# Forget-gate bias and causal mask by vector passes, and a planner that sees whole PSUM banks

## The chip, the cores and the metric

The kernel runs on one core of one Trainium2 chip. The metric is the time of one execution on the device in microseconds; the kernel before takes 2558.85 us, the median of three runs between 2553.24 and 2562.44. One further execution was profiled, and all rows below are from it.

## What is computed

One inference step of a four-layer encoder for 512 prompt frames and 64 sample frames side by side (576 columns), with a model width of 1024 and 16 heads of 64. Layer 0 and layer 3 mix with a gated linear recurrence, layer 1 with sliding-window attention (SWA) with a relative bias, layer 2 with "forgetting" attention (FoX). Each layer ends in a squared-ReLU feed-forward network (FFN) of width 4096. The change is about the scores of FoX:

```
logf = log_sigmoid(proj_f + b_f)
c    = cumsum(logf)                                   # per head, along the frames
s    = einsum('bqhd,bshd->bhqs', q, k) * SCALE
s    = s + c[q] - c[k]                               # forget bias: a column for the query, a row for the key
s    = where(kpos <= qpos, s, -inf)                  # causal mask
p    = softmax(s);  o = p @ v
```

The sample's 64 frames see 128 cached keys and their own 64, with a running sum of their own.

## The kernel before

Activations lie as 128 features by frames. Each projection is a sum of three fp32r products (high times high, high times low, low times high), so weights arrive by DMA as fp32 (`ws`), ACT rounds them to `wh`, and DVE or POOL forms the rest `wl`. A projection step is 24 products into one PSUM bank.

The program doesn't issue instructions directly. Every operation is recorded by `Plan.add` (L241) with its operands, and at the end `Plan.run` and `Plan.simulate` (L335) put all of them in an order by a list schedule: each operation has a latest time derived from the order of PE's products, a cost from `Plan.cost` (L280), possible engines (`alts`), and predecessors. A predecessor is an earlier operation that touched overlapping bytes of the same tile: `Plan.region` (L233) gives partitions and columns, so two operations on different columns of one PSUM bank are independent in the plan. PE may take a product up to 48 places ahead. `Plan.emit` (L459) issues each operation; this is why nearly all rows of the trace name line 471. The framework below adds the semaphores.

PSUM has eight banks, two for each of the names `pm`, `s`, `t` and `pv`. During attention, projections use `pm` alone, `s` takes scores, `t` transposes, `pv` the values. Attention runs beside the projections of later heads: each time so much projection time has passed (4320 ns in FoX), `_att` (L1581) takes one step, and a unit passes through four of them: its score products (`qk`), then maximum (`mx`), exponential (`ex`) and scaling (`sc`), then transposes and their copies (`transp`, `tevac`), then the value products (`av`). On PE one step makes a block: the scores of a new unit, the transposes of the unit two steps older, the values of the one three steps older.

FoX (`fox`, L1899) has eight head pairs with three units each, named after their query blocks of 128: unit (3) with 512 keys for each of two heads; unit (2, 0) with 384 and 128 keys for each head, side by side in one bank per head; unit (1) with 256 keys for each head and the sample's 256 columns for both heads in the first bank. In `qk` (L2033) each region is opened by a product of four rows, `CL` times `CR` (`cl`, `cr` in the trace; the cumulative sums as high and low parts, and ones), which writes c[q] - c[k]; for the sample `SL` times `SR` with six rows. Then come three score products, and an identity times `cmr` adds the mask on the last 128 columns. The row operands come from a DRAM scratch (`crow`) by six small DMAs a pair (`prep`, L1998) and are rounded to fp32r in `prep2` (L2009). `mx` (L2059) reduces each region from PSUM to its negated maximum on DVE; `ex` (L2067) reads PSUM again for the exponential with a running sum; `sc` scales head 0 on DVE and head 1 on POOL.

SWA (`unit`, L1766) adds its bias in another way: one DVE instruction reads the scores from PSUM and the bias from SBUF, writes the sum to SBUF and gives its maximum (`CUSTOM_DVE_ANT_0` in the trace, with a read of the accumulator after it).

Of the kernel before, what the change touches and what calls it, by code (L numbers as in the profile page):

```python
# [7 lines left out]
F32 = mybir.dt.float32  # L8
F32R = mybir.dt.float32r
# [122 lines left out]
class Engine:  # L132
# [5 lines left out]
    def __getattr__(self, op):  # L138
        core, load, names = self._c, self._l, self._names

        def call(out, *a, **k):
# [15 lines left out]
            core.plan.add([(e, op) for e in names], out, a, k, outs, ins, n)  # L157
# [3 lines left out]
class Queue:  # L161
# [3 lines left out]
    def dma_start(self, out, src):  # L165
# [8 lines left out]
        self._c.plan.add([("sync", "dma_start")], out, (src,), {}, [out], [src], n)  # L174


class Core:
# [8 lines left out]
    def any(self, *names):  # L186
        return Engine(self, *names)

# [23 lines left out]
class Item:  # L212
    __slots__ = ("alts", "out", "a", "k", "n", "pe", "pred", "succ", "tiles", "late", "at", "wait", "end", "seq", "func", "r32", "cols")


class Plan:
# [24 lines left out]
    def add(self, alts, out, a, k, outs, ins, n):  # L241
        o = Item()
        o.alts, o.out, o.a, o.k, o.n, o.seq = alts, out, a, k, n, len(self.items)
# [9 lines left out]
        for x, w in rw:  # L253
# [6 lines left out]
            p0, p1, runs = self.region(x)  # L260
# [19 lines left out]
    def cost(self, o, alt):  # L280
        e, op = alt
# [9 lines left out]
        if op == "scalar_tensor_tensor":  # L291
            return 1.85 * n + 90.0
        return (6.8 if op == "reciprocal" else 1.35) * n + 100.0
# [41 lines left out]
    def simulate(self):  # L335
# [15 lines left out]
        def offer(o):  # L351
            for e, _ in o.alts:
                cand[e].append(o)
# [17 lines left out]
        while left:  # L371
# [7 lines left out]
            again = True  # L379
            while again:  # L380
                again = False
                for e in names:
# [8 lines left out]
                    for o in cand[e]:  # L391
                        if e == "tensor" and o.seq > last:
                            continue
                        if o.at > now:
                            soon = o.at if soon is None else min(soon, o.at)
                            continue
                        k = (o.late + (1500.0 if o.func and o.func != func[0] else 0.0), o.seq)
# [10 lines left out]
                    if len(o.alts) > 1 and e == "gpsimd":  # L408

                        v = max(free["vector"], now) + self.cost(o, o.alts[0])  # L410
                        for x in cand["vector"]:
                            if x is not o and x.at <= now and x.late <= o.late and gets(x):
                                v += self.cost(x, x.alts[0])
                        if v <= now + c:
                            soon = max(free["vector"], now + 50.0)
                            heapq.heappush(heap, (soon, count, None))
                            count += 1
                            continue
# [1901 lines left out]
```

## Time and profile before

| | before |
|---|---|
| median of three runs | 2558.85 us |
| profiled execution: time, span | 2560.35 us, 2558.6 us |
| mean granted clock of the tensor engine | 0.983 |
| PE, PE weight loads | 98%, 95% of the span |
| DVE, ACT, POOL | 67%, 47%, 40% |
| DMA | 213 MB, 83 GB/s on average |

PE is the tensor engine's products, PEld its weight loads, DVE the vector engine, ACT the scalar engine, POOL GpSimd, SP the engine whose queue issues all DMAs. A share of the whole span says little about one stage, so the stages are read from views of stretches. A row of the timeline gives the start of the first instruction of a group, the time to the end of its last, what it computes, and in brackets the idle time before it and what released it. Starts are what to compare: products overlap, so that one lasts about 0.3 us while the next begins 0.1 us after it.

### The profile page before, as it was taken

The page shows a single profiled execution, that of the slowest core. Times are in us where ns is not written, and L with a number is a line of the kernel's source. Part 1 is how long each engine was busy: PE and PEld are TensorE (multiplying, and loading weights), DVE is VectorE, ACT ScalarE, POOL GpSimd, SP SyncE. Part 2 cuts the span into 40 slices and gives each one's busy share as a digit, 9 for nine tenths or more (in the row PEclk, how much of TensorE's full clock was granted, in tenths as well). Part 3 has the DMA queues.
Part 4 walks back from the last instruction along what each step waited for, and adds up shares of the span by engine and source line. Part 5 has one row for each costly group of instructions (what it writes and reads, how often), then busy time and mean ns, then how long its engine had stood idle before and what let it go on. Part 6 is the DMA issues. An engine that isn't in the chain of part 4 may idle for free. (4 is left out here: it accounts for less than half of the span.)

```text
span 2558.6 us, 47679 instructions
## 1 busy us (share of the span) xinstructions
PE 2503.4 (98%) x18897; PEld 2442.8 (95%) x18897; DVE 1711.8 (67%) x2835; ACT 1207.4 (47%) x2648; POOL 1015.9 (40%) x1084
## 2 busy tenths in 40 slices
PE   9999999999999999999999999999999999999998
PEld 9999999998789999999888889999999999999998
DVE  7776658676667575586643357586596796576584
ACT  6854435344554353463533334353463784353461
POOL 5644325343333252364312123253263763253260
PEclk9999999999999999999989889999999999999998
DMA  5135223242121222232321121232241231222231
GB/s 184 59 117 94 89 83 108 75 132 76 56 71 42 67 96 82 88 125 78 92 63 50 57 80 34 66 100 83 83 142 59 70 103 60 67 100 83 83 100 38
DMA packets 72687, 213.18 MB, mean 83 GB/s; under 512 B 9512, under 2 KB 24224, under 8 KB 72464
## 3 DMA queue, kind: packets, MB, share of 16 engines
q1 hardware_dynamic: 72464, 210.14, 26.5%
q8 instruction: 148, 2.42, 0.4%
q14 instruction: 75, 0.61, 0.1%
HBM read 199.16 MB, written 10.95 MB: 82 GB/s over the span
## 5 line engine op out<-in xcount | busy, mean ns | idle before, releaser
L471 DVE TENSOR_TENSOR wl<-ws,wh 128x512 fp32r<-128x512 f32 x548 | 476.3, 883 | 151.2 <-ACT wh L471 114.7
L471 ACT ACTIVATE wh<-ws 128x512 fp32r<-128x512 f32 x684 | 412.8, 625 | 322.2 <-PE pv L471 83.0
L471 POOL TENSOR_TENSOR q<-u 128x288 f32<-128x288 f32 x256 | 222.0, 872 | 259.1 <-ACT u L471 258.9
L471 POOL TENSOR_TENSOR wl<-ss,wh 128x512 fp32r<-128x512 f32 x72 | 117.6, 1634 | 501.5 <-PE pv L471 227.3
L471 POOL TENSOR_TENSOR wl<-ws,wh 128x512 fp32r<-128x512 f32 x136 | 202.5, 1495 | 212.6 <-ACT wh L471 142.3
L471 ACT ACTIVATE wh<-ss 128x512 fp32r<-128x512 f32 x192 | 119.7, 630 | 206.4 <-DVE ss L471 86.0
L471 PE MATMUL pm<-xh,wh 128*128 128x288 f32 x688 | 206.8, 301 | 0.2 <-DVE ol L471 0.2
L471 PE MATMUL pm<-xh,wl 128*128 128x288 f32 x688 | 205.5, 299 | 0.0
L471 PE MATMUL pm<-xl,wh 128*128 128x288 f32 x688 | 205.4, 299 | 0.0
L471 PE MATMUL pm<-hl,wh 128*128 128x288 f32 x520 | 154.0, 296 | 0.3 <-DVE hl L471 0.2
L471 PE MATMUL t<-hl,wh 128*128 128x288 f32 x520 | 153.5, 295 | 0.4 <-DVE hl L471 0.4
L471 PE MATMUL t<-hh,wl 128*128 128x288 f32 x520 | 153.8, 296 | 0.0
L471 PE MATMUL t<-hh,wh 128*128 128x288 f32 x520 | 153.6, 295 | 0.0
L471 PE MATMUL pm<-hh,wh 128*128 128x288 f32 x520 | 153.6, 295 | 0.0
L471 PE MATMUL pm<-hh,wl 128*128 128x288 f32 x520 | 153.4, 295 | 0.0
L471 PE MATMUL t<-xh,wh 128*128 128x288 f32 x504 | 149.6, 297 | 1.2 <-ACT xh L471 1.2
L471 PE MATMUL t<-xl,wh 128*128 128x288 f32 x504 | 149.6, 297 | 0.2
L471 PE MATMUL t<-xh,wl 128*128 128x288 f32 x504 | 149.1, 296 | 0.0
L471 PE MATMUL s<-hh,wl 128*128 128x288 f32 x504 | 149.0, 296 | 0.0
L471 PE MATMUL s<-hl,wh 128*128 128x288 f32 x504 | 148.8, 295 | 0.2 <-DVE hl L471 0.2
L471 PE MATMUL pv<-hh,wh 128*128 128x288 f32 x504 | 148.8, 295 | 0.0
L471 PE MATMUL pv<-hh,wl 128*128 128x288 f32 x504 | 148.7, 295 | 0.0
(434 smaller groups left out, 8801.1 us busy)
## 6 DMA issues: line engine op xcount, KB each, us to landing
ws<-w SPq DMA_DIRECT2D x365, 512.0 KB
toep_d<-toep SPq DMA_DIRECT2D x1, 3064.0 KB
res<-x SPq DMA_DIRECT2D x8, 288.0 KB
o_fxk<-kf SPq DMA_DIRECT2D x8, 288.0 KB
bt<-toep_d SPq DMA_DIRECT2D x16, 128.0 KB
o_fxv<-v SPq DMA_DIRECT2D x16, 128.0 KB
o_y<-res SPq DMA_DIRECT2D x2, 576.0 KB
o_y<-res SPq DMA_DIRECT2D x4, 288.0 KB
```

Source lines behind the costliest of these rows:

```text
L471: getattr(getattr(self.nc, e), op)(real(o.out), *[real(x) for x in o.a], **{n: real(x) for n, x in o.k.items()})
```

## The change

1. FoX: the bias products and the mask products go. The negated cumulative sums are written to DRAM once and loaded per pair as rows spread over 128 partitions (`nb`: two of 512 columns, one of 256), and the queries' sums are transposed once into columns (`cq`). In `qk`, ACT or POOL writes `nb` plus the column of `cq` into the unit's `pt`, and POOL adds the mask there. `mx` becomes the instruction of SWA: scores plus `pt` into `pt`, with the maximum, and a small negation. `ex` then reads `pt` from SBUF in place of PSUM.
2. The plan: for a PSUM operand, any access covers all partitions and all columns of its tile.
3. The plan: some operations may go to other engines than before (copies DVE or ACT; scaling DVE, ACT or POOL; squares ACT or POOL), an operation with a choice is put off where another of its engines would end it sooner, and the cost figures are new.

```diff
+    def copy(self, out, x):
+        self.alt(out, ("vector", "tensor_copy", (x,), {}), ("scalar", "activation", (x, AF.Copy), {}))
+    def add_col(self, out, x, col):
+        self.alt(out, ("scalar", "activation", (x, AF.Identity), {"bias": col}),
+                 ("gpsimd", "tensor_tensor", (x, col.to_broadcast(list(out.shape))), {"op": ALU.add}))
+    def mul_col(self, out, x, col):
...
+    def square(self, out, x):
...
@@ Plan.add
-            p0, p1, runs = self.region(x)
+            p0, p1, runs = (0, P, [(0, 1 << 20)]) if x.space == PSUM else self.region(x)
@@ Plan.cost
-            return 1.02 * n + 110.0 + (95.0 if "accum_out" in o.k else 0.0)
+            return 1.02 * n + (100.0 if o.bank else 130.0) + (190.0 if "accum_out" in k else 0.0)
-            return 2.5 * n + 120.0 if op == "tensor_tensor" else 1.2 * n + 100.0
+            return 2.7 * n + 120.0 if op == "tensor_tensor" else 1.2 * n + 120.0
...
-        return (6.8 if op == "reciprocal" else 1.35) * n + 100.0
+        if o.bank:
+            return 1.2 * n + 110.0
+        return (1.85 if op == "scalar_tensor_tensor" else 1.45) * n + 110.0
@@ tevac
-        self.nc.scalar.activation(u["pt"][0][:, :n[0]], u["t"][0][:, :n[0]], AF.Copy)
-        self.nc.vector.tensor_copy(u["pt"][1][:, :n[1]], u["t"][1][:, :n[1]])
+        for h in range(2):
+            self.nc.copy(u["pt"][h][:, :n[h]], u["t"][h][:, :n[h]])
@@ fox, ftask
+            nc.sync.dma_start(crow[:, 0:TP], ng[:16, :])
+            nc.sync.dma_start(crow[:, TP:768], ngs[:16, :256])
...
+            def tq():
+                g.append(self.paux())
+                for t in range(5):
+                    src = cc[:16, P * t:P * t + P] if t < 4 else lc[:16, 0:P]
+                    nc.tensor.transpose(g[0][:, 16 * t:16 * t + 16], src, self.ident[:16, :16])
+            self.later(tq, lc[:16, :P])
+            while not g:
+                yield
@@ prep
+            nb[p] = [self.slot("nb") for _ in range(2)] + [self.half("nbs")]
             for h in range(2):
-                nc.sync.dma_start(raw[0][c0:c0 + 2, :TP], two[h, :, :TP])
-                nc.sync.dma_start(raw[1][c0 + 2:c0 + 4, :TP], two[h, :, :TP])
...
+                row = crow[2 * p + h:2 * p + h + 1]
+                nc.sync.dma_start(nb[p][h][:, :TP], row[:, :TP].to_broadcast([P, TP]))
+                nc.sync.dma_start(nb[p][2][64 * h:64 * h + 64, :256], row[:, TP:768].to_broadcast([64, 256]))
@@ qk
-                            nc.tensor.matmul(o[h], CL[cb, qb], CR[cb, :w], start=True, stop=False)
-                            nc.tensor.matmul(o[h][:, w - P:], identr, cmr[:, 0:P], start=False, stop=True)
-                        nc.tensor.matmul(o, SL[cb, :P], SR[cb, :256], start=True, stop=False)
-                        nc.tensor.matmul(o[:, P:], identr, cmr[:, P:256], start=False, stop=True)
...
+                            nc.add_col(d, nb[p][h][:, :w], cq[:, j:j + 1])
+                            d, m = d[:, w - P:], cm[:, 0:P]
+                        nc.gpsimd.tensor_tensor(d, d, m, op=ALU.add)
@@ mx, ex
-                        nc.vector.tensor_reduce(nm[:, i:i + 1], u["s"][h][:, c0:c0 + w], axis=mybir.AxisListType.X,
-                                                op=ALU.max, negate=True)
+                        nc.vector.tensor_tensor_reduce(d, u["s"][h][:, c0:c0 + w], d, 1.0, NEG, ALU.add, ALU.max,
+                                                       accum_out=top[:, i:i + 1])
+                    nc.vector.tensor_scalar(nm[:, :len(ops)], top[:, :len(ops)], -1.0, None, op0=ALU.mult)
-                        nc.scalar.activation(pt[h][:, c0:c0 + w], u["s"][h][:, c0:c0 + w], AF.Exp, bias=nm[:, i:i + 1],
+                        nc.scalar.activation(pt[h][:, c0:c0 + w], pt[h][:, c0:c0 + w], AF.Exp, bias=nm[:, i:i + 1],
```

## Rows read from the trace of the kernel before

**Rows 1.** The page, part 1: busy us, share of the span, instructions of each engine.

```profile
PE 2503.4 (98%) x18897; PEld 2442.8 (95%) x18897; DVE 1711.8 (67%) x2835; ACT 1207.4 (47%) x2648; POOL 1015.9 (40%) x1084
```

**Rows 2.** Busy time by stretch: FoX, then sliding-window attention; last columns clock, DMA, GB/s.

```profile
1240.00:1530.00 290.00, 275.25 (x2049) 242.48 (x2049) 133.02 (x274) 113.57 (x305) 63.53 (x95) 0.91 0.19 60
...
590.00:760.00 170.00, 154.35 (x1279) 138.34 (x1278) 107.87 (x390) 83.94 (x276) 63.75 (x105) 0.96 0.20 61
```

**Rows 3.** Timeline of PE in a block of unit (2, 0).

```profile
1347.11 0.44 PE L471 MATMUL s<-cr,cl 4*128 4x384 f32 x2
1347.48 0.44 PE L471 MATMUL s<-kh,qh 64*128 64x384 f32 x2
...
1348.57 0.33 PE L471 MATMUL s<-cr,cl 4*128 4x128 f32 x2
1349.54 0.33 PE L471 MATMUL s<-kh,qh 64*128 64x128 f32 x2 [0.65 <-DVE nm L471]
...
1350.63 0.33 PE L471 MATMUL s<-kh,ql 64*128 64x128 f32 x1 [0.55 <-DVE nm L471]
```

**Rows 4.** Timeline of DVE in the same block.

```profile
1348.92 0.56 DVE L471 TENSOR_REDUCE nm<-s 128x1 f32<-128x384 f32 x1 [5.44 <-PE s L471]
1350.02 0.56 DVE L471 TENSOR_REDUCE nm<-s 128x1 f32<-128x384 f32 x1 [0.54 <-PE s L471]
```

**Rows 5.** Waits of PE (us in total, times, longest): FoX, then sliding-window attention.

```profile
PE s L471 <- DVE nm L471: 12.0, 21, 0.7
PE s L471 <- ACT pt L471: 2.0, 3, 0.7
...
PE s L471 <- DVE mx L471: 9.4, 20, 0.8
```

**Rows 6.** Timeline of PE in a block of unit (3).

```profile
1338.57 0.50 PE L471 MATMUL s<-cr,cl 4*128 4x512 f32 x2
1339.00 0.50 PE L471 MATMUL s<-kh,qh 64*128 64x512 f32 x2
...
1339.88 0.44 PE L471 MATMUL s<-cmr 128*128 128x128 f32 x2
1340.16 1.06 PE L471 MATMUL t<-ident,pt 128*128 128x128 f32 x8
```

**Rows 7.** Timeline of PE in a block of unit (1) with the sample, without a stop.

```profile
1328.92 0.38 PE L471 MATMUL s<-cr,cl 4*128 4x256 f32 x2
1329.23 0.39 PE L471 MATMUL s<-kh,qh 64*128 64x256 f32 x2
...
1329.78 0.44 PE L471 MATMUL s<-cmr 128*128 128x128 f32 x2
1330.15 0.38 PE L471 MATMUL s<-sr,sl 6*128 6x256 f32 x1
1330.46 0.55 PE L471 MATMUL s<-kcs,qs 128*128 128x128 f32 x3
```

**Rows 8.** Busy time by stretch: block of unit (3), after the block of rows 3, later.

```profile
1338.50:1342.20 3.70, 3.70 (x37) 2.65 (x35) 2.34 (x4) 1.79 (x5) 0.80 (x1) 1.00 0.60 213
1353.50:1355.50 2.00, 2.00 (x11) 1.99 (x10) 1.03 (x2) 0.09 (x1) 0.95 (x2) 0.50 0.00 0
1356.00:1358.00 2.00, 2.00 (x19) 2.00 (x18) 0.00 (x0) 0.00 (x0) 0.00 (x0) 1.00 0.19 66
```

**Rows 9.** Groups by form in FoX: busy us, mean ns, idle before and releaser.

```profile
L471 ACT ACTIVATE pt<-s,nm 128x256 f32<-128x256 f32 x24 | 11.2, 470 | 18.6 <-PE s L471 13.8 <-DVE nm L471 4.7
...
L471 DVE TENSOR_REDUCE nm<-s 128x1 f32<-128x256 f32 x24 | 9.4, 421 | 22.1 <-PE s L471 20.0 <-ACT pt L471 2.1
...
L471 POOL TENSOR_TENSOR pt<-pt,den 128x256 f32<-128x256 f32 x8 | 5.2, 656 | 23.6 <-DVE den L471 23.6
```

**Rows 10.** Groups by form in sliding-window attention.

```profile
L471 DVE CUSTOM_DVE_ANT_0 pt<-s,bt 128x256 f32<-128x256 f32 x48 | 18.8, 421 | 13.6 <-PE s L471 11.7 <-POOL qs L471 1.4
...
L471 DVE DVE_READ_ACCUMULATOR2_ANT mx<- 128x1 f32 x80 | 6.6, 82 | 0.0
```

More of the change, by code (lines that the diff above doesn't have):

```diff
@@ L156, in call @@
             load.account(outs, ins, end, name)
-            core.plan.add([(e, op) for e in names], out, a, k, outs, ins, n)
+            core.plan.add([(e, op, a, k) for e in names], out, outs, ins, n)
         return call
@@ L212 @@
 class Item:
-    __slots__ = ("alts", "out", "a", "k", "n", "pe", "pred", "succ", "tiles", "late", "at", "wait", "end", "seq", "func", "r32", "cols")
+    __slots__ = ("alts", "out", "n", "bank", "pe", "pred", "succ", "tiles", "late", "at", "wait", "end", "seq", "func", "r32", "cols")
 class Plan:
@@ L239, in region, with add @@
         return p0, p1, Load.region(None, x)[1]
-    def add(self, alts, out, a, k, outs, ins, n):
+    def add(self, alts, out, outs, ins, n):
         o = Item()
-        o.alts, o.out, o.a, o.k, o.n, o.seq = alts, out, a, k, n, len(self.items)
+        o.alts, o.out, o.n, o.seq = alts, out, n, len(self.items)
+        a, k = alts[0][2:]
+        o.bank = any(x.space == PSUM for x in ins)
         o.pe = alts[0][0] == "tensor"
@@ L280, in cost @@
     def cost(self, o, alt):
-        e, op = alt
+        e, op, _, k = alt
         n = o.n
@@ L407, in simulate @@
                     c = self.cost(o, alt)
[L408 to L416, printed above, removed]
+                    if len(o.alts) > 1:
+                        wait = None
+                        for y in o.alts:
+                            f = y[0]
+                            if f == e:
+                                continue
+                            v = max(free[f], now) + self.cost(o, y)
+                            if v <= now + c:
+                                for x in cand[f]:
+                                    if x is not o and x.at <= now and x.late <= o.late and gets(x):
+                                        v += self.cost(x, next(z for z in x.alts if z[0] == f))
+                            if v < now + c or v == now + c and f == "vector":
+                                wait = max(free[f], now + 50.0)
+                                break
+                        if wait is not None:
+                            heapq.heappush(heap, (wait, count, None))
                             count += 1
+                            skip.add((e, o))
+                            again = True
                             continue
@@ L1303, in copy @@
         def copy(out, src, n):
[L1304 to L1307 removed]
+            nc.copy(out, src)
         def uev(m):
```

119 lines of the change are left out of this document (59 added, 60 removed).

## Prediction

> **What bounds the kernel now.** I read the page first: the tensor engine, PE, is busy for 2503.4 of 2558.6 us [rows 1], so 55.2 us of idle time are all that a better order alone can give, besides work taken away and clock won back. Then the busy time by stretch: of those 55.2 us, the sliding-window attention stage holds 170 - 154.4 = 15.6 and the FoX stage 290 - 275.3 = 14.8; in the same two the granted clock is 0.96 and 0.91 of full speed [rows 2]. The rest, 24.8 us, is spread over the other 2100 us. So the two attention stages are where something can be won, and in both PE is still the bound: in FoX, VectorE (DVE) is busy 133 us of 290, ScalarE (ACT) 114, GpSimd (POOL) 64.
>
> The timeline of PE then shows what an attention block between two projections looks like. In the block of unit (2, 0) PE starts the bias pair of the 384-column region, its products, the mask pair, the bias pair of the 128-column region, and then stands twice, 0.65 and 0.55 us, "released by DVE nm" [rows 3]. The timeline of DVE says why: the reduction of the first region in one bank runs from 1348.92 to 1349.48, that in the other from 1350.02 to 1350.58, and PE starts its next product into that bank 0.05 to 0.06 us later [rows 3, 4]. PE waits for a reader of other columns of the bank that it is about to write. The planner compares columns, sees no conflict, and puts the reduction ahead of the remaining products; the program's semaphores make PE wait. The list of waits has 24 such stops in FoX (12.0 + 2.0 us) and 20 with "DVE mx" in the sliding-window stage (9.4 us) [rows 5].
>
> **Products taken away.** Per head pair 18 products go (8 bias, 8 mask, one bias and one mask for the sample), 144 in all. I take each pair's price from start to start of its group and the next. Unit (3): 1339.00 - 1338.57 = 0.43 and 1340.16 - 1339.88 = 0.28, together 0.71 us [rows 6]. Unit (2, 0): 0.37 for the 384-column bias [rows 3], 0.37 for a mask pair that another bias follows (1330.15 - 1329.78, [rows 7]), and 0.28 each for the 128-column bias (the wait hides its own price; the 128-column mask pair is nearest) and the last mask: 1.30. Unit (1) with the sample: 0.31 + 0.37 + 0.31 [rows 7] and half of 0.28 for a single mask: 1.13. That is 3.14 us a pair, 25 us for eight. Bounds: the 3968 columns that go per pair at the pace of an undisturbed stretch (19 products of 256 columns in 2.00 us, [rows 8]: 0.41 ns a column) would be 1.6 us a pair, 13 in all; above, 27, since some of them ran at the lower clock. I take 25, which is read directly.
>
> **Waits.** With a bank counted as a whole, the reduction can't be placed between two products of its bank: it follows the last one, on DVE, and PE doesn't meet it. All 44 stops are of this kind by their releaser, 23.4 us. Each also costs the refilling of the pipe: 1349.54 - 1348.57 = 0.97 less 0.28 for the pair is 0.69 against 0.65 of idle time. With 0.06 each I take 26 us, with bounds of 18 (a third of them come back elsewhere) and 28.
>
> **Clock.** Two levels are granted, 1.0 (2.4 GHz) and 0.5 (1.2 GHz). A mean of 0.91 over 290 us is 52 us at the lower one, 0.96 over 170 is 14, 66 together [rows 2]. At the lower level 11 products start in 2 us, at the upper 19 [rows 8], so 42% of such time is lost: 28 us. Behind the two stops of [rows 3] a stretch runs at 0.50, while the block of unit (3), which has transposes and value products but no stop, keeps 1.00 throughout [rows 6, 8]. So I expect most falls to go with the stops and take three quarters, 21 us; the bounds are 0 and 28.
>
> One rule speaks against this. The Trainium skill (TensorE: Matmul & The Clock Gate, Part 4: PE-mode transpose) says that transposes don't count as activity for the clock gate; by it the transposes in each block would pull the clock down whether or not PE stopped, and the sum would be 21 us smaller. The undisturbed block of unit (3), with its eight transposes at 1.00, speaks for the stops instead.
>
> **What is added.** For each of 72 regions: bias plus cq (ACT or POOL), the mask on 128 columns (POOL), and in place of the reduction a pass that adds the bias and takes the maximum. That pass exists in the sliding-window stage: 421 ns for 256 columns from PSUM, the reduction of today also 421, plus 82 for reading its accumulator [rows 9, 10]: 72 x 0.08 = 6 us on DVE. The bias adds are 2816 columns a pair, 11 x 0.470 [rows 9] = 5.2 us, 41 us if all are on ACT, which idles for 176 of 290. The masks are at most 72 x 0.656 = 47 us on POOL, idle for 226. None of it needs a product of PE, so it can run before its block; I cost it at nothing on PE. If that cover were gone it is the chain of the fourth case. The exponential now reads SBUF, so the banks come free one step earlier. What leaves: the casts and the row operands.
>
> **Queues.** On SP's queue the six small row loads a pair become four broadcast loads of 640 KB together. At the 213 GB/s that the queues carried beside a block [rows 8] that is 3.0 us a pair of 36 us. The loads are issued two units ahead; a weight load queued behind them is late by up to these 3 us, and with a mean of 60 GB/s in the stage [rows 2] the queue has room to make that up: nothing. The five transposes for cq and the wait for them let attention start one or two pumps later, with projections running meanwhile; it returns as units left over at the end. I take 3 us, from 0 to 6. Products, copies and squares that get another engine, and the new cost figures, act where PE is already full: nothing, and at best a third of the 24.8 us outside, 8.
>
> **Sum.** 25 + 26 + 21 - 3 = 69 us. The profiled execution took 2560.35, 1.5 above the median of the runs, so 2560 - 69 = 2491, and by the median 2490 us.
>
> **Rivals.**
> First, the clock stays as it is: the falls belong to the blocks with their small products, not to the stops. Then 25 + 26 - 3 = 48: 2511 us. For it: falls lie only in attention stages. Against: unit (3).
> Second, the plan doesn't do what it says, and PE waits as long as before: the maximum now starts only after the bank's last product and a vector-built operand, and PE meets it at the next block's products into the same two banks or at the transposes. Then the clock stays too: 25 - 3 = 22, 2537 us. It takes a maximum that ends a whole block late, some 235/24 = 9.8 us after its products (235 is the FoX stage less its 55 of the sum); for four regions of 256 columns it takes 4 x (421 + 82) ns = 2 us. Against it.
> Third, slower: the vector chain of a unit (bias, mask, maximum, exponential, scaling) becomes the bound of FoX. Transposes come two blocks after the products, so it decides from 2 x 9.8 = 19.6 us; from there each us costs 24 us, and after the 69 won the change is slower by 0.3% from 19.6 + 77/24 = 22.8. At 23.6 it would be 2490 + 96 = 2586 us. What the rows give is 2.0 + 4 x 0.470 + 4 x 0.656 = 6.5 us plus hand-overs [rows 9, 10]; it would have to queue three times as long as it works. The Trainium skill (SBUF — State Buffer, Who interferes with whom) says that a DVE instruction with two SBUF inputs and a GpSimd instruction that reads SBUF block one another; the added masks would meet the weight subtractions of DVE, which is how such a queue could grow. No row here separates the two.
>
> **Chances and range.** Forecast 0.70, clock stays 0.16, waits stay 0.10, slower 0.03, some other loss near today's time 0.01. Low end: 27 + 28 + 28 - 0 and 8 from elsewhere is 91, or 2468. The high end takes in the second figure, 2511, and half of the way from there to the waits that stay: 2526. Left out: the third and fourth cases and some 0.05 beyond the ends. A change within 0.3%, about 8 us, can't be told from none here; faster than that are the first three cases all but a remnant, 0.95; the same 0.02; slower 0.03.
>
> **What would show it.** In the changed profile: no waits of PE for "DVE nm", "mx" or "top" in either stage; no products from cl, cr, sl, sr or cmr; a mean clock in FoX of 0.97 or more, and a stage of about 235 us instead of 290. If the waits go and the clock stays near 0.91, the first rival is right; if PE waits at transposes for pt, the third. The forecast falls if PE's stops move to other releasers in like number.

## The result and the profile after

The changed kernel takes 2461.53 us (median of four runs, 2460.81 to 2461.68) against 2559.77 for the kernel before: a ratio of 0.9619, 95% interval [0.9601, 0.9638], 98 us less. The forecast was 2490 us with a range from 2468 to 2526. The sign and the three mechanisms of the gain were right. A fourth term, put down as a small loss, turned out to be a gain, and with it the time lies below the range.

The page, part 1, against [rows 1] (all calls go through one helper, which stands at L518 here and at L471 before):

```profile
PE 2431.0 (99%) x18758; PEld 2395.3 (97%) x18758; DVE 1645.6 (67%) x2840; ACT 1309.4 (53%) x2914; POOL 917.7 (37%) x1019
```

The span is 2459.9 us, so PE's idle time fell from 55.2 to 28.9 us, and its busy time by 72.4 us. The first is the waits; the second holds both the products taken away and the clock.

To compare stages I bound them by products that all kernels have: the sliding-window stage from its first score product to the 25th product of the next FFN (its first into a bank of `t`), FoX from the transpose of the forget gate to the last product with a cached value. Busy time by stretch between these marks (PE, PEld, DVE, ACT, POOL busy with their counts, then clock, DMA share, GB/s), first the kernel before:

```profile
622.90:916.10 293.20, 279.10 (x2231) 262.61 (x2231) 192.65 (x523) 128.34 (x362) 102.59 (x139) 0.98 0.19 58
1241.20:1528.90 287.70, 273.39 (x2031) 240.91 (x2033) 131.31 (x270) 112.74 (x302) 62.99 (x94) 0.91 0.19 59
```

and the changed kernel:

```profile
627.90:894.80 266.90, 264.81 (x2231) 254.49 (x2231) 175.85 (x493) 151.46 (x419) 84.02 (x112) 1.00 0.20 64
1217.70:1431.80 214.10, 214.05 (x1882) 198.37 (x1884) 114.92 (x327) 142.37 (x365) 94.44 (x180) 1.00 0.33 103
```

FoX loses 73.6 us: PE stands for 0.05 us of 214 where it stood for 14.3, and the clock is full where it was 0.91. The sliding-window stage, whose code is the same, loses 26.3 us.

The timeline of PE in a block of unit (3) and one of unit (2, 0), which answer to [rows 6] and [rows 3]:

```profile
1297.44 0.50 PE L518 MATMUL s<-kh,qh 64*128 64x512 f32 x2
...
1298.34 1.09 PE L518 MATMUL t<-ident,pt 128*128 128x128 f32 x8
...
1305.42 0.44 PE L518 MATMUL s<-kh,qh 64*128 64x384 f32 x2
1305.70 0.34 PE L518 MATMUL s<-kl,qh 64*128 64x384 f32 x2
1305.88 0.34 PE L518 MATMUL s<-kh,ql 64*128 64x384 f32 x2
1306.05 0.22 PE L518 MATMUL s<-kh,qh 64*128 64x128 f32 x2
1306.11 0.28 PE L518 MATMUL s<-kl,qh 64*128 64x128 f32 x2
1306.22 0.27 PE L518 MATMUL s<-kh,ql 64*128 64x128 f32 x2
1306.43 0.88 PE L518 MATMUL t<-ident,pt 128*128 128x128 f32 x6
```

No bracket, so no idle time. The scores of unit (2, 0) take 1.01 us from start to the first transpose where they took 4.06 (1347.11 to 1351.17 in the block of [rows 3]); those of unit (3) take 0.90 where they took 1.59 [rows 6]. VectorE in the same block, against [rows 4]:

```profile
1306.63 0.56 DVE L518 CUSTOM_DVE_ANT_0 pt<-s,pt 128x384 f32<-128x384 f32 x1 [4.22 <-PE s L518]
...
1308.13 0.17 DVE L518 TENSOR_SCALAR nm<-top 128x4 f32<-128x4 f32 x1
```

The first pass over a bank now follows the last product of the block (1306.22 + 0.27 = 1306.49). The maxima are done 1.6 us later, well ahead of the next block. Against [rows 5], the largest waits of PE that are left in the whole kernel are single ones in the recurrent layers; in the sliding-window stage there are 2.1 us, in FoX 0.05, and none in the list names `mx`, `nm` or `top`:

```profile
PE t L518 <- ACT gt L518: 2.1, 2, 1.1
PE s L518 <- ACT gt L518: 2.0, 1, 2.0
```

The added work in FoX, in groups by form, against [rows 9]:

```profile
L518 ACT ACTIVATE pt<-nb,cq 128x512 f32<-128x512 f32 x15 | 10.4, 713 | 0.0
...
L518 ACT ACTIVATE pt<-pt,nm 128x256 f32<-128x256 f32 x24 | 12.0, 502 | 2.0 <-DVE nm L518 1.9
...
L518 POOL TENSOR_TENSOR pt<-pt,cm 128x128 f32<-128x128 f32 x72 | 34.3, 489 | 33.9 <-ACT pt L518 32.8
...
L518 DVE CUSTOM_DVE_ANT_0 pt<-s,pt 128x256 f32<-128x256 f32 x24 | 9.2, 420 | 4.4 <-PE s L518 3.8 <-POOL pt L518 0.6
```

The pass with maximum takes 420 ns for 256 columns, as the 421 read from the sliding-window stage; the mask 489 ns, under the 656 taken for it; the exponential 502 ns from SBUF against 470 from PSUM.

### The profile page after: what moved, and what is told of

It is laid out like the page before. It is cut to its first block, busy times and chain, and to the rows that moved or that the text cites. A ratio compares the mean times of both kernels' runs of the same rounds, so it can differ in the third digit from the quotient of the medians.

```text
span 2459.9 us, 47410 instructions
## 1 busy us (share of the span) xinstructions
PE 2431.0 (99%) x18758; PEld 2395.3 (97%) x18758; DVE 1645.6 (67%) x2840; ACT 1309.4 (53%) x2914; POOL 917.7 (37%) x1019
## 4 chain that ended last, share of the span: by engine, by line
PE 89%; DVE 5%; issue 3%; ACT 1%; POOL 1%; DMA 1%; SPq 0%; POOLq 0%; DVEq 0%; ACTq 0%
PE pm L518 25%; PE s L518 24%; PE t L518 20%; PE pv L518 20%; DVE cv L518 1%; DVE t L518 1%; DVE G L518 1%; DVE wl L518 1%; DVE res L518 0%; ACT pt L518 0%; DMA prm<-prm 0%; DVE pt L518 0%; DMA ws<-w 0%; DVE h L518 0%; POOL gt L518 0%
## 5 line engine op out<-in xcount | busy, mean ns | idle before, releaser
L518 ACT ACTIVATE wh<-ws 128x512 fp32r<-128x512 f32 x684 | 410.5, 624 | 320.0 <-PE t L518 95.8
L518 DVE TENSOR_TENSOR wl<-ws,wh 128x512 fp32r<-128x512 f32 x513 | 423.7, 840 | 146.8 <-ACT wh L518 120.4
L518 POOL TENSOR_TENSOR wl<-ws,wh 128x512 fp32r<-128x512 f32 x171 | 260.0, 1527 | 227.8 <-ACT wh L518 142.3
L518 POOL TENSOR_TENSOR wl<-ss,wh 128x512 fp32r<-128x512 f32 x72 | 105.2, 1461 | 554.0 <-PE pm L518 295.8
L518 ACT ACTIVATE wh<-ss 128x512 fp32r<-128x512 f32 x192 | 119.7, 629 | 236.0 <-DVE ss L518 132.8
L518 PE MATMUL pm<-xl,wh 128*128 128x288 f32 x608 | 180.8, 297 | 0.4 <-DVE xl L518 0.4
L518 PE MATMUL pm<-xh,wh 128*128 128x288 f32 x608 | 181.2, 298 | 0.0
L518 PE MATMUL pm<-xh,wl 128*128 128x288 f32 x608 | 179.6, 295 | 0.0
L518 PE MATMUL s<-hl,wh 128*128 128x288 f32 x536 | 158.7, 296 | 0.0
L518 PE MATMUL s<-hh,wl 128*128 128x288 f32 x536 | 158.4, 296 | 0.0
L518 PE MATMUL s<-hh,wh 128*128 128x288 f32 x536 | 158.4, 296 | 0.0
L518 POOL TENSOR_TENSOR q<-u 128x288 f32<-128x288 f32 x100 | 87.9, 880 | 185.2 <-ACT u L518 182.4
L518 PE MATMUL t<-xh,wh 128*128 128x288 f32 x520 | 154.2, 297 | 0.9 <-ACT xh L518 0.8
L518 PE MATMUL t<-xl,wh 128*128 128x288 f32 x520 | 154.3, 297 | 0.4 <-DVE xl L518 0.2
L518 PE MATMUL t<-xh,wl 128*128 128x288 f32 x520 | 154.3, 297 | 0.0
L518 PE MATMUL pv<-hh,wl 128*128 128x288 f32 x512 | 151.1, 295 | 0.0
L518 PE MATMUL pv<-hh,wh 128*128 128x288 f32 x512 | 151.1, 295 | 0.0
L518 PE MATMUL pv<-hl,wh 128*128 128x288 f32 x512 | 151.0, 295 | 0.0
L518 PE MATMUL pm<-hh,wh 128*128 128x288 f32 x504 | 148.8, 295 | 0.0
L518 PE MATMUL pm<-hl,wh 128*128 128x288 f32 x504 | 148.8, 295 | 0.0
L518 PE MATMUL pm<-hh,wl 128*128 128x288 f32 x504 | 148.7, 295 | 0.0
L518 PE MATMUL t<-hh,wl 128*128 128x288 f32 x496 | 146.5, 295 | 0.0
```

The lines of the kernel that those rows point to most:

```text
L518: getattr(getattr(self.nc, e), op)(real(o.out), *[real(x) for x in a], **{n: real(x) for n, x in k.items()})
```

## The experiments

The stages of all kernels, in us of the span of the profiled execution, bounded as above (gates: up to the last product with `ch` in layer 3):

| kernel | start | window stage | to FoX | FoX | to gates | to end | median |
|---|---|---|---|---|---|---|---|
| before | 622.9 | 293.2 | 325.1 | 287.7 | 525.7 | 504.0 | 2559 |
| bank_only | 621.8 | 275.9 | 325.1 | 247.6 | 525.6 | 502.1 | 2501.08 |
| planner_only | 628.4 | 303.8 | 323.6 | 289.4 | 523.8 | 505.1 | 2574.15 |
| planner_bank | 628.0 | 267.0 | 324.3 | 247.1 | 525.4 | 505.3 | 2499.07 |
| after_products | 627.6 | 267.0 | 323.2 | 241.8 | 521.9 | 505.5 | 2487.95 |
| after | 627.9 | 266.9 | 322.9 | 214.1 | 522.4 | 505.7 | 2461.53 |
| after_no_bank | 629.4 | 303.5 | 322.7 | 225.3 | 522.1 | 504.9 | 2509.37 |
| products_no_bank | 628.5 | 303.5 | 323.0 | 278.9 | 522.3 | 504.0 | 2560.77 |

**The bank rule alone (bank_only).** The kernel before with one line of the plan:

```diff
-            p0, p1, runs = self.region(x)
+            p0, p1, runs = (0, P, [(0, 1 << 20)]) if x.space == PSUM else self.region(x)
```

Expected: 

> The kernel before with one line of the change: the plan counts a PSUM bank as a whole. Forecast's reasons: the 44 stops go (26 us) and the clock with them (21 to 28 us), 2560 - 47 to 54 = 2506 to 2513, although all 144 bias and mask products are still there. If the 28 us that the forecast missed belong to the bank rule as well: about 2478. If the clock falls belong to the blocks with their small products: 2534, with the granted clock in FoX still near 0.91.

Measured: 2501.08 us, 0.9767 [0.9753, 0.9782]. Busy time by stretch in the two stages:

```profile
621.80:897.70 275.90, 271.39 (x2231) 258.37 (x2231) 193.39 (x526) 128.63 (x361) 98.19 (x136) 0.99 0.20 62
1222.80:1470.40 247.60, 247.30 (x2033) 219.57 (x2035) 129.13 (x268) 111.08 (x302) 66.49 (x96) 0.99 0.22 69
```

All 144 products are still there (x2033 in FoX), and so are the transposes; the stops are gone, and the clock with them is back at 0.99. Read in steps of half a microsecond, the time at the lower level falls from 54.6 us in ten stretches to 3.4 in one (FoX), and from 13.7 in three to 6.8 in one (window stage). So the falls of the clock belonged to the stops, which ends the first rival: with all small products and transposes in place, one fall of ten is left in FoX. The sliding-window stage wins 17.3 us with no change of its code.

The two stages lose 57.4 us, of which 23.6 are idle time (14.31 and 14.10 us to 0.30 and 4.51). What the clock takes is read from starts of equal projection products in the kernel before, seven steps apart at 0.50 and then sixteen steps apart at 1.00:

```profile
1353.90 0.41 PE L471 MATMUL pm<-wh,xh 128*128 128x256 f32 x1
...
1355.39 0.41 PE L471 MATMUL pm<-wh,xl 128*128 128x256 f32 x1
...
1356.03 0.28 PE L471 MATMUL pm<-wl,xh 128*128 128x256 f32 x1
...
1357.92 0.28 PE L471 MATMUL pm<-wh,xh 128*128 128x256 f32 x1
```

That is 0.213 us a product against 0.118, so 45% of the time at the lower level is lost, and 58 us less of it are worth 26. The 7.6 us left over are neither idle time nor clock. A block of unit (2, 0) shows what they are. Its first transpose in the kernel before (the block of [rows 3], which starts at 1347.11), and such a block in bank_only:

```profile
1351.17 0.84 PE L471 MATMUL t<-ident,pt 128*128 128x128 f32 x6
```

```profile
1292.88 0.44 PE L471 MATMUL s<-cr,cl 4*128 4x384 f32 x2
...
1295.35 0.84 PE L471 MATMUL t<-ident,pt 128*128 128x128 f32 x6
```

The same 20 products, at full clock in both, take 4.06 us with the two stops and 2.47 without: 1.59 us for 1.20 us of idle time. A stop costs some 0.20 us beyond its idle time, which for 44 stops is about 9 us.

**The planner's other edits alone (planner_only), and with the rule (planner_bank).** The kernel before with parts 2 and 3 of the change and the old scores; planner_only leaves out the line above. The core of the common edit:

```diff
-                    if len(o.alts) > 1 and e == "gpsimd":
+                    if len(o.alts) > 1:
...
-            return 1.02 * n + 110.0 + (95.0 if "accum_out" in o.k else 0.0)
+            return 1.02 * n + (100.0 if o.bank else 130.0) + (190.0 if "accum_out" in k else 0.0)
...
-        self.nc.scalar.activation(u["pt"][0][:, :n[0]], u["t"][0][:, :n[0]], AF.Copy)
-        self.nc.vector.tensor_copy(u["pt"][1][:, :n[1]], u["t"][1][:, :n[1]])
+        for h in range(2):
+            self.nc.copy(u["pt"][h][:, :n[h]], u["t"][h][:, :n[h]])
```

Expected of planner_only: 

> The kernel before with the planner's other edits alone (engine choices for copies, scaling and squares, putting off, cost figures), columns of a bank still independent, FoX as before. Forecast's reasons: within 8 us of 2560, stops and clock as before. If the missed 28 us come from the better choice of engines: about 2532.

Expected of planner_bank: 

> The kernel before with all edits of the planner, bank rule included, and FoX with its bias and mask products as before. It differs from the changed kernel by the products and the vector passes alone. Forecast's reasons: 2461.5 + 25 - 3 = about 2484. If each product also costs its neighbours (a change from 4 or 128 rows to 64 and back): 2461.5 + 35 to 40 = 2497 to 2502.

Measured: planner_only 2574.15 us, 1.0052 [1.0035, 1.0069]; planner_bank 2499.07 us, 0.9762 [0.9748, 0.9777]. The waits of PE in planner_only:

```profile
PE s L518 <- DVE mx L518: 16.3, 34, 1.4
PE s L518 <- DVE nm L518: 13.6, 24, 0.7
```

With more freedom to place VectorE's work by columns, the plan makes 34 stops in the window stage instead of 20, and six falls of the clock (31 us at the lower level) instead of three. The stage is 10.6 us longer: there the better planner makes a slower order, while it is blind to the bank. Another 5.5 us of the whole difference lie in the start, which all kernels with these edits have longer. With the rule the same edits bring the window stage to 267.0 us, 8.9 below the rule alone, but the start is 6.2 us longer and the end 3.2, so that the net is 2 us.

**The products alone (after_products).** The changed kernel with the 144 products back at their old places, fed with zeros, so that they add nothing:

```diff
+                        for h in range(2):
+                            cb = slice(cbase(p, h), cbase(p, h) + 4)
+                            nc.tensor.matmul(o[h], zr[cb, :P], zr[cb, :w], start=True, stop=False)
...
+                        for h in range(2):
+                            nc.tensor.matmul(o[h][:, w - P:], zr[:, 0:P], zr[:, 0:P], start=False, stop=True)
```

Expected: 

> The changed kernel with 144 products put back in their old places, of zeros, so that they add nothing to the scores; the vector passes stay. What it loses against the changed kernel is the price of the products alone. Forecast's sum: 25 us, so 2487. If the neighbours pay too: 35 to 40 us, 2497 to 2502. If products of four rows pull the clock down: more than 45 us, with the granted clock in FoX below 0.97.

Measured: 2487.95 us, 0.9718 [0.9704, 0.9733]. FoX takes 241.8 us against 214.1; all other stages agree with the changed kernel within 0.5 us. So the products cost 26.4 us by the medians, 27.7 in the stage, against 25 in the forecast. And with them in place the vector form is 11.1 us faster than the old scores (planner_bank): 5.3 in FoX, 3.5 on the way to the gates of layer 3.

**The vector form without the rule (after_no_bank), and with the products too (products_no_bank).** The line of bank_only taken back, in the changed kernel and in after_products:

```diff
-            p0, p1, runs = (0, P, [(0, 1 << 20)]) if x.space == PSUM else self.region(x)
+            p0, p1, runs = self.region(x)
```

Expected of after_no_bank: 

> The changed kernel with the whole-bank line taken back; the vector form and the planner's edits stay. Theory A, the stops at a bank that VectorE still reads are in the order and not in the products: they come back in both attention stages and the clock falls with them, as between the two kernels with the planner's edits and the old products (2574.15 without the rule, 2499.07 with it): 75 us more, 2537 us, with the sliding-window stage near 304 us and the forgetting attention near 256. Theory B, the stops in the forgetting attention were owed to the many small products that filled a bank column by column, and the vector form cures them by itself: only the 37 us of the sliding-window stage come back, 2498 us, and the forgetting attention stays near 214 to 220 us.

Measured: 2509.37 us, 0.9809 [0.9788, 0.9831]. Waits of PE, then busy time in FoX:

```profile
PE s L518 <- DVE mx L518: 16.3, 34, 1.4
PE s L518 <- DVE top L518: 7.0, 10, 0.8
```

```profile
1255.60:1480.90 225.30, 217.82 (x1882) 199.35 (x1884) 117.64 (x335) 140.37 (x360) 94.22 (x177) 1.00 0.31 98
```

Nearer to theory B: the window stage takes the 303.5 us of planner_only, but FoX is only 11.2 us longer than with the rule and its clock is full. The timeline of PE in a block of unit (2, 0) shows one stop where [rows 3] has two:

```profile
1348.93 0.22 PE L518 MATMUL s<-kh,qh 64*128 64x128 f32 x2
1349.92 0.33 PE L518 MATMUL s<-kl,qh 64*128 64x128 f32 x2 [0.77 <-DVE top L518]
```

Whether the vector form or the missing products cured the rest was then the question. Expected of products_no_bank: 

> The changed kernel without the whole-bank line and with the 144 products back at their old places, fed with zeros. Without the rule alone the changed kernel takes 2509 us, with 10 stops of 0.7 us in the forgetting attention (225 us) and a full clock there; the old scores without the rule take 289 us in that stage. Theory A, the vector form frees the banks sooner and so cures the stops: the products cost their 26.5 us as they do with the rule, the stage takes about 253 us with some 10 stops and a full clock, the time is near 2536 us. Theory B, the products, each written ahead of or behind the others into columns of a bank, make the stops: some 20 stops and ten falls of the clock are back, the stage takes 275 to 289 us, the time 2558 to 2574 us.

Measured: 2560.77 us, 1.0005 [0.9995, 1.0015], with a FoX stage of 278.9 us: theory B. Waits of PE, its timeline in a block of unit (2, 0), and busy time in FoX and then behind that block:

```profile
PE s L518 <- DVE top L518: 13.8, 20, 0.8
```

```profile
1370.41 0.33 PE L518 MATMUL s<-kh,qh 64*128 64x128 f32 x2 [0.75 <-DVE top L518]
...
1371.62 0.47 PE L518 MATMUL s<-kh,ql 64*128 64x128 f32 x1 [0.67 <-DVE top L518]
```

```profile
1255.00:1533.90 278.90, 265.14 (x2024) 234.85 (x2025) 120.73 (x340) 141.91 (x358) 87.68 (x173) 0.91 0.26 79
...
1372.00:1374.00 2.00, 2.00 (x11) 1.65 (x10) 0.68 (x5) 0.38 (x1) 0.00 (x0) 0.50 0.00 0
```

The two stops a block are back, in six of the eight blocks of unit (2, 0), and behind these the clock of 0.50. The whole vector form and the planner's other edits together, without the rule and with the products, are worth nothing: the kernel takes the time of before. The four kernels make a table of medians (the kernel before, beside their runs, had 2557.96 to 2559.77):

| | without the rule | with the rule | the rule gives |
|---|---|---|---|
| with the products | 2560.77 | 2487.95 | 72.8 |
| without them | 2509.37 | 2461.53 | 47.8 |
| taking them away gives | 51.4 | 26.4 | both 99.2 |

Of the 99.2 us, 26.4 need the products' removal whatever the plan does, 47.8 the rule whatever the products do, and 25.0 come from either.

**How much is chance of the order (after_jit1, after_jit2, planner_bank_jit, after_products_jit).** One constant in the plan's estimate of a product, 11.0 in after_jit1 and 12.0 in the other three:

```diff
-            return max(n / 2.4 + 11.5, 110.0 if o.cols > 64 else 56.0) if o.r32 else max(4 * n / 2.4, 4 * 27.0) + 11.5
+            return max(n / 2.4 + 12.0, 110.0 if o.cols > 64 else 56.0) if o.r32 else max(4 * n / 2.4, 4 * 27.0) + 11.5
```

Expected of after_jit1: 

> The changed kernel with one figure of the planner moved that has no meaning of its own: 11.0 ns instead of 11.5 ns added to each product's estimated time. It asks how much of a difference between two orders is chance of the planner. Theory A, the order is robust and a difference of 10 to 15 us between two variants is owed to the edit: the time stays within 3 us of 2461.5. Theory B, any small shift makes another order, and stages move by 3 to 6 us with it: the time lies 5 to 15 us off, more likely above.

Expected of after_jit2: 

> The same with 12.0 ns instead of 11.5. Theory A: within 3 us of 2461.5. Theory B: 5 to 15 us off, and not by the same stages as with 11.0.

Expected of planner_bank_jit: 

> The old scores with the planner's edits and the whole-bank rule (2499.1 us), with 12.0 instead of 11.5 ns added to each product's estimated time. If the 11 us between this kernel and the changed one with its products put back are chance of the order, this lies several us off, at 2488 to 2494 or above 2503; if they are the vector form's, within 3 us of 2499.

Expected of after_products_jit: 

> The changed kernel with the 144 products put back (2488.0 us), with 12.0 instead of 11.5 ns added to each product's estimated time. If the 11 us are the vector form's, within 3 us of 2488 and again 8 us or more below the kernel with the old scores and the same figure; if they are chance, the two come within 5 us of each other.

Measured: after_jit1 2468.21 us, 0.9650 [0.9626, 0.9673], 6.7 above the changed kernel; after_jit2 2462.72, 0.9630 [0.9602, 0.9657], 1.2 above; planner_bank_jit 2497.40, 0.9764 [0.9744, 0.9785]; after_products_jit 2488.62, 0.9727 [0.9710, 0.9745]. Of the 6.7 us of after_jit1, 5.3 lie in the start (633.2 us instead of 627.9), where one wait of PE is longer than any that the changed kernel has there (2.0 us):

```profile
PE t L518 <- DVE yl L518: 3.9, 1, 3.9
```

So some 7 us, most of it in the start, can be chance. FoX is 1.4 and 0.7 us longer in these two than in the changed kernel. The second pair differs by 8.8 us where the first differed by 11.1, again 5.0 in FoX (245.1 and 240.1) and 2.6 on the way to the gates: what the vector form gives beyond its products recurs, and is not chance of the order alone.

**The cover of the vector work (after_dve2).** Two needless passes of VectorE between each maximum and its exponential:

```diff
+                        for _ in range(2):
+                            nc.vector.tensor_scalar(d, d, 1.0, None, op0=ALU.mult)
```

Expected: 

> The changed kernel with two needless passes of VectorE behind each addition with maximum (a multiplication by 1, in place): some 0.4 to 0.8 us each, 72 groups of scores, so 60 to 85 us more of VectorE in the forgetting attention, 1 to 4 us more for each unit between its last product and its exponentials. It puts a price on the cover of the vector form. Theory A, the forecast's: this work lies beside the products of the neighbouring units, VectorE has 99 of 214 us to spare, and the time stays within 5 us of 2461.5. Theory B, the vector chain is nearly the bound already (the rival of the forecast that ends slower): the stage grows by half of the added work or more, 2490 to 2545 us, with waits of TensorE for the probabilities.

Measured: 2463.52 us, 0.9633 [0.9609, 0.9656], 2.0 above the changed kernel. The largest group of the added passes, GpSimd's weight subtractions in the stage, and the busy time of all engines there:

```profile
L518 DVE TENSOR_SCALAR pt<-pt 128x256 f32<-128x256 f32 x48 | 21.9, 497 | 0.1
```

```profile
L518 POOL TENSOR_TENSOR wl<-ws,wh 128x512 fp32r<-128x512 f32 x33 | 44.5, 1359 | 22.3 <-ACT wh L518 19.6 <-PE pv L518 1.9 <-POOL wl L518 0.6
```

```profile
1218.60:1436.40 217.80, 216.23 (x1888) 199.47 (x1890) 160.27 (x448) 143.15 (x369) 126.18 (x199) 1.00 0.32 102
```

Some 69 us of work were added (21.9, 21.4, 13.7 and 12.2 in the four largest groups). The plan moved 23 weight subtractions to GpSimd (10 to 33), VectorE rose by 45 us, and FoX by 3.7. The vector chain is far from being the bound; the third rival is ruled out with a dose.

**Single edits of the planner (after_oldcost, after_fixed, after_square_pool, after_oldrule).** Each is the changed kernel with one edit taken back: the old cost figures; fixed engines for the evictions of the transposes and for the scaling; the squares of the FFN on their old engine (the expectation calls them squares of the recurrent gates; they are the squared ReLU); the old rule for putting work off:

```diff
-            return 1.02 * n + (100.0 if o.bank else 130.0) + (190.0 if "accum_out" in k else 0.0)
+            return 1.02 * n + 110.0 + (95.0 if "accum_out" in k else 0.0)
...
-            self.nc.copy(u["pt"][h][:, :n[h]], u["t"][h][:, :n[h]])
+        self.nc.scalar.activation(u["pt"][0][:, :n[0]], u["t"][0][:, :n[0]], AF.Copy)
...
-                    nc.square(q["q"], u())
+                    eng.tensor_tensor(q["q"], u(), u(), op=ALU.mult)
...
-                    if len(o.alts) > 1:
+                    if len(o.alts) > 1 and e == "gpsimd":
```

Expected of after_oldcost: 

> The changed kernel with the planner's old cost figures; the choices of engine, the whole-bank rule and the vector form stay. Two stretches moved with the planner's edits and were not in the forecast: the start up to the sliding-window attention, 622 us without these edits and 628 us in every kernel that has them, and the sliding-window stage, 276 us with the bank rule alone and 267 us with the planner's edits beside it. Theory A, the new figures misplace work in the first recurrent layer: the start falls to 622 us, the window stage stays near 267, and the time is near 2455 us. Theory B, the figures bring the better order in the window stage: that stage is near 276 us and the time near 2470 us. If both hold, the time is near 2464. If the engine choices do both, nothing moves: 2461 to 2462 us.

Expected of after_fixed: 

> The changed kernel with the evictions of the transposed probabilities fixed again (head 0 on ScalarE, head 1 on VectorE) and the scaling by the row sum fixed again (head 0 VectorE, head 1 GpSimd). Theory A, the free choice of engine in the attention gave the 9 us of the sliding-window stage between the bank rule alone (275.9 us) and the bank rule with the planner's edits (267.0 us): that stage is near 276 us and the forgetting attention grows by some us too, time 2470 to 2475 us. Theory B, that gain is the cost figures': nothing moves, 2461 to 2463 us. The start should stay at 628 us either way, since this edit doesn't touch the recurrent layers.

Expected of after_square_pool: 

> The changed kernel with the squares of the recurrent gates on the engine that they had before, instead of a choice between ScalarE and GpSimd. Theory A, the squares that now fall to ScalarE delay the gate evictions there, for which TensorE waits in the first recurrent layer (2.0 us in the profile of the changed kernel, and a lower busy share of TensorE between 50 and 150 us): the start falls from 628 to about 622 us, the time to about 2455. Theory B, the start is longer through the cost figures alone: the start stays at 628 us and the time at 2461 to 2462.

Expected of after_oldrule: 

> The changed kernel with the old rule of the planner for work that may go to several engines: the first free engine takes it, and only GpSimd weighs whether the first engine on the list would be done earlier; the lists of engines and the cost figures of the change stay. Neither old cost figures nor squares or evictions on fixed engines took back the 6 us that the start up to the sliding-window attention lost (622 to 628 us). Theory A, that loss is the new rule's: the start falls to 622 us, and the time to 2455 us if the rest stays. Theory B, the start depends on the whole of the order and no single edit has it: the start stays between 626 and 633 us, and the other stages lose some us too, as in the two kernels with one edit undone: 2465 to 2478 us.

| kernel | start | window stage | to FoX | FoX | to gates | to end | median | ratio |
|---|---|---|---|---|---|---|---|---|
| after | 627.9 | 266.9 | 322.9 | 214.1 | 522.4 | 505.7 | 2461.53 | 0.9619 |
| after_oldcost | 629.2 | 270.5 | 325.7 | 216.8 | 523.4 | 509.3 | 2478.41 | 0.9694 [0.9674, 0.9714] |
| after_fixed | 627.8 | 272.0 | 322.6 | 216.9 | 522.2 | 506.0 | 2470.41 | 0.9663 [0.9643, 0.9683] |
| after_square_pool | 632.3 | 267.2 | 326.5 | 214.3 | 527.5 | 507.0 | 2477.11 | 0.9688 [0.9669, 0.9708] |
| after_oldrule | 629.8 | 266.6 | 322.7 | 215.2 | 522.1 | 505.9 | 2466.29 | 0.9643 [0.9619, 0.9667] |

No edit taken back brings the start down to 622 us: theory A fell for the cost figures, the squares and the rule for putting off. The old cost figures lose 1 to 4 us in each of the six stretches, 17 by the medians, and theory B's window stage of 276 us didn't come (270.5). The fixed evictions and scaling give back 5.1 us of the window stage, with waits of PE for `ol` (the split of attention's output on VectorE) of 3.4 us instead of 0.9. The squares tell most plainly. GpSimd's one group in after_square_pool:

```profile
L518 POOL TENSOR_TENSOR q<-u 128x288 f32<-128x288 f32 x256 | 222.2, 874 | 260.5 <-ACT u L518 257.5 <-PE s L518 1.5 <-PE t L518 1.5
```

and the changed kernel's two:

```profile
L518 POOL TENSOR_TENSOR q<-u 128x288 f32<-128x288 f32 x100 | 87.9, 880 | 185.2 <-ACT u L518 182.4 <-DMA ws<-w 1.3 <-PE pm L518 0.3
...
L518 ACT ACTIVATE q<-u 128x288 f32<-128x288 f32 x156 | 66.3, 433 | 0.8
```

156 of 256 squares take half the time on ScalarE, which has the room. Without that, the two stretches that hold the FFNs of layers 1 and 2 are 3.6 and 5.1 us longer. Another 4.4 us of this kernel lie in the start, where chance moves as much. All four come out slower than the changed kernel, by 5 to 17 us, and the smallest of these is within what half a nanosecond did. No variant was faster than the changed kernel.

## Why the forecast was too small

Along the path before, bank_only, planner_bank, after_products, after, the gain of 97.7 us (2559.23, the median of before beside these runs, less 2461.53) falls into four terms:

| term | forecast | measured on this path |
|---|---|---|
| waits and clock (bank rule) | 26 + 21 = 47 | 58.2 |
| planner's other edits | 0, at best 8 | 2.0 |
| vector form beside its products, with the late start | -3 (-6 to 0) | 11.1 (8.8 in the second pair) |
| products taken away | 25 (13 to 27) | 26.4 |

**Where it was right.** What bounds: the two attention stages, and there the stops at a bank that VectorE still reads. The mechanism of the rule (the reduction follows the last product and PE doesn't meet it) stands in the timeline after. The products were priced to 1.4 us by starts read directly; by columns at full pace they would have been put at little more than half. The three rivals fell: the clock went with the stops (bank_only), the waits didn't come back under other names, the vector chain took 69 us more work at a cost of 2 to 4. But FoX was expected at about 235 us, 55 less, and came to 214, 73.6 less; the sliding-window stage gave 26.3.

**The vector form was bounded on the wrong side: this step failed.** The step is "I take 3 us, from 0 to 6". It looked for a loss only. The forecast named what could bring a gain, the banks that come free a step earlier and the casts and row operands that leave, and put neither into the sum nor into the range. The form gives 9 to 11 us with its products in place, and 13.4 without the rule (planner_only less products_no_bank). Even with all other terms as measured, a loss of 3 in its place would have left the time within the range.

About 5 of the 11 are in FoX: attention's own products, those put back included, take 97.4 us from start to start in after_products and 100.4 in planner_bank, and ten fewer projection products fall within the stage (1075 and 1085). Most of these 3 us (2.3) lie in the blocks of the first head pair. Its unit (2, 0) in planner_bank, from the first product to the first projection behind it, and in after_products:

```profile
1236.61 0.44 PE L518 MATMUL s<-cr,cl 4*128 4x384 f32 x1
...
1240.57 0.55 PE L518 MATMUL pm<-xl,wh 128*128 128x288 f32 x1
```

```profile
1237.24 0.44 PE L518 MATMUL s<-zr 4*128 4x384 f32 x2
...
1239.71 0.35 PE L518 MATMUL pm<-xl,wh 128*128 128x288 f32 x1
```

In the first, PE takes one head's products of the 384-column region and then the other's, without a wait, and needs 3.96 us, the last 0.7 at the lower clock; in the second it alternates (x2) and needs 2.47. The pair's unit (1) takes 3.22 and 2.37. The second couple of kernels repeats it with no fall of the clock (3.70 and 2.48, 3.22 and 2.38). From the second head pair on, the blocks of unit (2, 0) take 2.46 to 2.48 us in planner_bank and 2.47 to 2.56 in after_products. So the gain there is not a bank that comes free earlier in each block, and PE's waits in the stage, 0.88 and 0.16 us, leave little room for one. That the first pair's row operands come late would fit, since both kernels with the old scores wait once for `cl` just before these blocks (0.9 and 0.7 us), but it wasn't tested. Some 3 us are on the way to the gates of layer 3: planner_bank waits there once for `acc` (1.5 us) and once for `gt` (2.3), after_products twice for `gt` (2.1 in all); why, stays open.

**The clock was cut by a quarter without a row for it.** Of ten falls in FoX one is left in bank_only, of three in the window stage one, and 58 of 68 us at the lower level are gone. That is worth 26 us instead of 21; in the changed kernel FoX has no fall left at all. The price was also read too low: the counts in [rows 8], 11 and 19, are products under way in each stretch, of which 9 and 17 start there. From start to start the loss is 45% and not 42%, the upper bound of the clock 30 us and not 28, and the lower bound of the products 15 and not 13. Against the rule of the Trainium skill (TensorE: Matmul & The Clock Gate, Part 4: PE-mode transpose), that transposes don't count as activity for the clock gate, the runs are plain on its effect here: the changed kernel has all of its transposes and a clock of 1.00 over the 214 us of FoX.

**A stop costs more than it stands.** The forecast added 0.06 us of refilling to each of 44 stops, read behind the first of two. The whole block gives 0.20 us a stop at full clock, so that waits cost some 32 us where 26 were taken and 28 was the upper bound. Waits and clock together, 58.2, passed the sum of the stated bounds, 28 + 28 = 56.

**"Nothing" for the planner was a balance.** The net of 2 us is -8.9 in the window stage, +6.2 in the start and +3.2 at the end. The choice of engine for evictions and scaling holds 5.1 of the 8.9; the start is owed to no single edit tried, and lies between 627 and 633 us in all kernels with these edits, against 622 to 623 in the two without. Why, stays open.

**The two large terms are not independent.** The forecast priced the rule in the kernel before, with the products in place, and most of the products from blocks or groups without a stop, as if the rule already held; in that order the terms add up, and no gain was counted twice. But it didn't say so. (Its high end, half of the way from 2511 to 2537, is 2524 by its own sum and not 2526.) By the same prices the products alone, without the rule, would have been put at 25 us, and they give 51.4; the rule on top of that gives 47.8 instead of 72.8.

**Contention.** By the second page that the forecast named, the Trainium skill (SBUF — State Buffer, Who interferes with whom), VectorE's instructions with two SBUF inputs and GpSimd's reads block one another. With GpSimd busy for 94 us of FoX instead of 63, VectorE's weight subtraction there takes 799 ns on average instead of 754, about 1.8 us over its 39, off PE's path; GpSimd's own takes 1403 ns instead of 1413. The effect, if it is this, is small.

## What to carry to other kernels

A planner has to see a resource in the unit in which the semaphores guard it: finer knowledge (columns of a bank) let it place readers where PE then stood, and giving the same planner more freedom made it worse until the unit was right. Where an edit removes instructions and another removes the stops between them, price each with the other in and out, since part of the gain (25 us here) belongs to either. And move one meaningless constant of the scheduler before differences of a few microseconds between two orders are given a cause: here that alone moved 1 to 7 us.

## What the runs showed of the hardware

- Not each stop lowers the clock. In FoX of products_no_bank each of the six blocks with two stops is followed by a fall, and of the eight with one stop three; after_no_bank has one stop of 0.6 to 0.8 us in each of ten blocks, no fall, and a granted clock of 1.00 throughout. In the window stage of both, 34 stops go with six falls. What decides between them the runs don't show.
- A stop costs more than its idle time. The same 20 products took 4.06 us with stops of 0.65 and 0.55 us and 2.47 us without, at full clock: some 0.20 us more a stop.
- The price of a product depends on what stands around it: the last low product of the 128-column regions (64 rows, 128 columns) took 530 ns from start to start on average in the kernel before, where seven of sixteen ran into a stop, and about 112 ns in bank_only; a transpose 157 ns, part of them at the lower clock, and 121 ns.
- A square of 288 columns takes 433 ns on ScalarE and 880 on GpSimd, so a list of engines is only as good as the cost figure beside each.
